# A hybrid encoder layer: attention stores begun by another engine, V laid out by pairs of heads, far results by heads, the gate from tanh

## The chip, the cores and the metric

The kernel runs on one core of one Trainium2 chip. A core has five engines with an instruction queue each, worked off in order: TensorE (PE; matmuls, its weight loads shown as PEld), VectorE (DVE), ScalarE (ACT), GpSimd (POOL) and SyncE (SP, which here only begins transfers). They wait for one another through semaphores. Sixteen DMA engines move the data; a transfer is begun by an instruction in the queue of SP, ScalarE or GpSimd. The metric is the time of one execution on the device in microseconds, lower is better.

## The reference

One layer over x (2048 positions by 1024), float32, weights and mem (256 by 1024) given:

```python
def reference(x, mem, ...):                       # one layer (DEPTH = 1)
    y = rmsnorm(h, norm_mix_g) @ w_in             # 1024 -> q 512, k 512, v 512, a 512, g 512
    q, k = partial_rotary(q), partial_rotary(k)   # 8 heads of 64
    att = dilated_sliding_attention(q, k, v)
    conv = conformer_conv(a, g, conv_w, conv_b, conv_ln_g, conv_ln_b)
    h = h + concatenate([att, conv]) @ w_out
    h = h + cross_attention(rmsnorm(h), rmsnorm(mem)) @ w_xo
    h = h + square(relu(rmsnorm(h) @ w_up)) @ w_down
    return rmsnorm(h, norm_final_g)

# dilated_sliding_attention: three patterns (128, 1), (512, 4), (2048, 16): every d-th
# position, a band of 64 to either side; outputs mixed by the softmax of their log-denominators
# conformer_conv: u = a * sigmoid(g); depthwise convolution of 31 taps + bias; layernorm; silu
```

## The kernel before, in words

Matmuls in full precision are three products of high and low halves (`mm3`, L197 to L200): a value is rounded by ScalarE to the high half, the rest is subtracted by VectorE or GpSimd. So one weight tile means a load of 512 KB, a cast on ScalarE (L189), a subtraction (L190), and 24 matmuls of 128x512 per output tile.

The order of the program is this. First mem is projected and x is normalised and transposed, all in 512-position quarters n or p. Then the input projection follows, unit by unit: `glu(c, ns)` makes channels c of the gated values (a ScalarE sigmoid of g at L508, a VectorE product with a at L511, stored to `uscr`), `lin_qk` stores q and k to scratch in DRAM, and `lin_v` writes V: for each 128 positions and each half g of the heads a tile `vst` of 4 heads x 130 numbers (64 high, two ones, 64 low) goes to the scratch `vtok`, whose rows are 8 x 130 half-precision numbers. `edges` writes zero rows ahead of it and behind it.

Then comes the *far stretch*: the attention of the first quarter, `att(0, p2_)`. There `att_far` does the distance-16 pattern for all 2048 positions, head by head, and `att_units` the two near patterns (distance 4, then distance 1) of the first quarter; heads go in pairs `pr`, `hh` is the head within a pair. One unit is: scores (PE, L855/L856 or L992), mask and row minimum (DVE, L772), Exp (ACT, L773), transposition (PE, L779), cast to a high part `ph` (ACT, L782), low part `pl` (DVE, L783), product with V (PE, L787 to L789). The units are woven as a pipeline by `att` and `weave`, with the gates of the other half of the positions (`glu(c, (2, 3))`, in `rest`) and the conv layernorm of the first quarter, whose Silu is at L266, between them. The far results (64 numbers, denominator, minimum: ROW = 66) go from `o2` to `oscr[pr][1]` once per half head, those of distance 4 from `os_` to `oscr[pr][0]` once per pair; both stores stand in ScalarE's queue (`nc.scalar`). `combine` loads both into `ld`, mixes the three patterns (mostly on GpSimd, at the end on VectorE) and transposes the result for the output projection.

After the far stretch the rest of the layer (`post(p)`: output projection, cross-attention, MLP, final norm) runs quarter by quarter, and beside it, woven in by step rates (0.95 and 0.6 a step), the near attention `att(p + 1)` and the convolution `conv(p + 1)` of the next quarter; `load_v` then loads a pattern's V tile for the next pair as soon as the old one is used up, in the far stretch all three at once after the last near unit of a pair. In the near-only quarters `turned` reorders q on GpSimd (L820).

The order on the engines is made by the framework when the program is built, from its own estimate of the times (`schedule_with_timeline_sim`); `after` and `pinned` fix parts of it: what is traced within a pinned generator is issued behind the last instruction recorded for that engine, so TensorE's order follows the order in which the generators are traced. Tiles with the same tag share buffers; a tile waits for the last reader of its buffer, a store among them. `o1` has one buffer in `aq`, and in the far stretch a second one for even pairs.

Of the kernel before, what the change touches and what calls it, by code (L numbers as in the profile page):

```python
# [10 lines left out]
F32 = mybir.dt.float32  # L11
# [10 lines left out]
P = 128  # L22
# [25 lines left out]
def hybrid_layer(ctx, tc, A, out):  # L48
# [61 lines left out]
    vtok = dr.tile([256 + S + 256, VR], F16, name="vtok")  # L110
# [3 lines left out]
    oscr = [[dr.tile([S, 2 * ROW], F32, name=f"oscr{p}_{q}") for q in (1, 2)] for p in range(4)]  # L114
# [30 lines left out]
    def setup():  # L145
# [14 lines left out]
        ACT.copy(cw.rearrange("p a b -> p (a b)"), pv[:, 64:192])  # L160
# [330 lines left out]
    def glu(c, ns, fine=False):  # L491

        sig = {}

        def unit(x, c0):
# [5 lines left out]
            for n in ns:  # L501
# [4 lines left out]
                if x == "g":  # L506
                    sig[n] = t2(f"sig{c}_{n}")
                    ACT.activation(sig[n], pt, AF.Sigmoid)  # L508
                else:
                    u = t2(f"u{c}_{n}")  # L510
                    last["dve"] = DVE.tensor_tensor(u, pt, sig[n], op=ALU.mult)  # L511
# [32 lines left out]
    def lin_v(g, ns):  # L544
# [18 lines left out]
        for t in range(4 * ns[0], 4 * ns[-1] + 4):  # L563
# [272 lines left out]
    def att_far(p2_, h, k, vt, q):  # L836
# [5 lines left out]
        def unit(rq, qh, ql):  # L842
# [40 lines left out]
    def combine(p, pr, o0):  # L883
# [63 lines left out]
    def att_units(p, far, then):  # L947
# [8 lines left out]
        def load_v(pr, pats):  # L956
            es = slice(pr * 2 * VW, (pr + 1) * 2 * VW)
            if 2 in pats and far:
                vt[2] = far.tile([P, 16, 2 * VW], F16, tag="v3", name=f"v3_{pr}")
                dma(vt[2], vtok[256:256 + S, es].rearrange("(i r) e -> i r e", r=16))  # L960
            if 0 in pats:
                vt[0] = aq.tile([P, 5, 2 * VW], F16, tag="v1", name=f"v1_{p}{pr}")
                for c in range(5):
                    t0 = 256 + 512 * p + P * c - 64
                    dma(vt[0][:, c], vtok[t0:t0 + P, es].rearrange("(i r) e -> r i e", r=16))
            if 1 in pats:
                vt[1] = aq.tile([P, 4, 2, 2 * VW], F16, tag="v2", name=f"v2_{p}{pr}")
# [467 lines left out]
```

## Time and profile before

| | |
|---|---|
| median of 3 runs | 2909.81 us (2908.92 to 2911.87) |
| the profiled execution | 2913.75 us, its span 2912.0 us |
| busy: PE, PEld | 2840.1 us (98%), 2383.9 us (82%) |
| busy: DVE, ACT, POOL | 1860.9 us (64%), 1185.7 us (41%), 456.9 us (16%) |
| DMA packets, bytes | 622,271, 433.73 MB; 553,817 of them under 2 KB, 191,269 under 512 B |
| mean granted TensorE clock | 0.990 |

The span is the time from the first to the last instruction; the execution's time holds some 2 us more. Busy time of PE is modelled from pipelined matmuls, so a busy PE is not PE at its peak. The granted clock is the share of full speed that TensorE was given. A wait is put down to what ended it last; "ACTq" and "SPq" are the instruction queues of ScalarE and SyncE where they begin a transfer.

### The profile page before, as it was taken

What the parts mean: (1) busy time and instruction counts of PE and PEld (TensorE: products, weight loads), DVE (VectorE), ACT (ScalarE), POOL (GpSimd) and SP (SyncE); (2) the same over time, 40 slices, a digit from 0 to 9 for tenths busy, and PEclk for the clock granted to TensorE, in tenths of its full rate; (3) what the DMA queues carried; (4) which work ended last, traced back from release to release, by engine and by line L of the source; (5) the groups of instructions that cost most, each with busy time, mean ns of one, the idle gap of its engine ahead of it and who ended that gap; (6) DMA issues with size and microseconds to landing.
All of it is one profiled execution on the core that took longest, in us unless ns stands there. A gap on an engine that the chain in (4) does not pass through costs nothing.

```text
span 2912.0 us, 41370 instructions
## 1 busy us (share of the span) xinstructions
PE 2840.1 (98%) x15628; PEld 2383.9 (82%) x15628; DVE 1860.9 (64%) x3311; ACT 1185.7 (41%) x2002; POOL 456.9 (16%) x502
## 2 busy tenths in 40 slices
PE   8989999989899999999999999999999999999999
PEld 7878899877688888888878888888888888888888
DVE  5636536455679886566887856589886555544445
ACT  5623211566444433433543334344333433432233
POOL 1336421121101111200021122001111200000000
PEclk9999999999899999999999999999999999999999
DMA  8979854798834544545344545534543445233332
GB/s 264 301 153 226 199 138 135 176 231 214 203 113 131 138 126 125 171 143 173 111 135 126 148 115 171 177 116 126 137 126 112 141 130 180 88 94 94 99 96 73
DMA packets 622271, 433.73 MB, mean 149 GB/s; under 512 B 191269, under 2 KB 553817, under 8 KB 622072
## 3 DMA queue, kind: packets, MB, share of 16 engines
q1 hardware_dynamic: 566904, 408.81, 50.1%
q10 hardware_dynamic: 55168, 22.29, 3.3%
q8 instruction: 123, 2.02, 0.3%
q14 instruction: 76, 0.62, 0.1%
HBM read 339.89 MB, written 91.11 MB: 148 GB/s over the span
## 4 chain that ended last, share of the span: by engine, by line
PE 82%; DVE 7%; DMA 4%; ACT 2%; issue 2%; SPq 1%; POOL 0%; ACTq 0%; POOLq 0%; DVEq 0%
PE dn L198 8%; PE dn L199 8%; PE dn L200 8%; PE up L198 7%; PE up L200 7%; PE up L199 7%; PE lin L198 3%; PE lin L199 3%; PE lin L200 3%; PE xs L198 2%; PE xs L200 2%; PE xs L199 2%; DVE cacc L215 2%; PE o L198 2%; PE o L199 2%
## 5 line engine op out<-in xcount | busy, mean ns | idle before, releaser
L199 PE MATMUL dn<-hhl,whi_d 128*128 128x512 f32 (+1 forms) x1056 | 402.9, 384 | 1.4 <-DVE hhl L1309 1.4
L198 PE MATMUL up<-mh,whi_u 128*128 128x512 f32 x1024 | 402.7, 393 | 0.8 <-DVE rl L1306 0.5
L198 PE MATMUL dn<-hhh,whi_d 128*128 128x512 f32 (+1 forms) x1056 | 401.6, 391 | 1.1 <-ACT hhh L1308 1.1
L200 PE MATMUL dn<-hhh,wlo_d 128*128 128x512 f32 (+1 forms) x1056 | 402.1, 384 | 0.0
L199 PE MATMUL up<-ml,whi_u 128*128 128x512 f32 x1024 | 399.7, 390 | 1.8 <-DVE ml L1199 1.8
L200 PE MATMUL up<-mh,wlo_u 128*128 128x512 f32 x1024 | 399.8, 391 | 0.0
L215 DVE SCALAR_TENSOR_TENSOR cacc<-cu,cw,cacc 128x512 f32<-128x512 f32 x480 | 388.8, 810 | 5.5
L189 ACT CAST whi_d<-raw_d 128x1024 fp32r<-128x1024 f32 x128 | 134.6, 1052 | 423.5 <-PE up L199 383.0
L1324 DVE TENSOR_TENSOR h<-h,dn 128x512 f32<-128x512 f32 (+1 forms) x264 | 172.3, 667 | 161.0 <-PE dn L200 159.7
L189 ACT CAST whi_u<-raw_u 128x1024 fp32r<-128x1024 f32 x128 | 134.4, 1050 | 327.6 <-PE dn L199 293.4
L1306 DVE SCALAR_TENSOR_TENSOR rl<-up,ssumx 128x512 f32<-128x512 f32 x128 | 88.0, 690 | 259.6 <-PE up L200 255.5
L198 PEld LDWEIGHTS dn<-hhh,whi_d 128*128 128x128 f32 x1056 | 197.7, 188 | 40.6 <-DVE h L1324 3.5
L200 PEld LDWEIGHTS dn<-hhh,wlo_d 128*128 128x128 f32 x1056 | 198.4, 188 | 39.3
L199 PEld LDWEIGHTS dn<-hhl,whi_d 128*128 128x128 f32 x1056 | 198.8, 188 | 37.8 <-DVE hhl L1309 2.3
L199 PEld LDWEIGHTS up<-ml,whi_u 128*128 128x128 f32 x1024 | 192.4, 188 | 41.1 <-DVE ml L1199 3.1
L200 PEld LDWEIGHTS up<-mh,wlo_u 128*128 128x128 f32 x1024 | 192.2, 188 | 40.1
L198 PEld LDWEIGHTS up<-mh,whi_u 128*128 128x128 f32 x1024 | 192.4, 188 | 39.2 <-DVE rl L1306 0.9
L773 ACT ACTIVATE sm<-sm,o 128x256 f32<-128x256 f32 (+1 forms) x384 | 160.3, 465 | 119.1 <-DVE o L772 107.4
L190 DVE TENSOR_TENSOR wlo_u<-raw_u,whi_u 128x1024 fp32r<-128x1024 f32 x128 | 162.6, 1270 | 28.7 <-ACT whi_u L189 28.4
L190 DVE TENSOR_TENSOR wlo_d<-raw_d,whi_d 128x1024 fp32r<-128x1024 f32 x128 | 160.1, 1251 | 23.7 <-ACT whi_d L189 23.5
L772 DVE CUSTOM_DVE_ANT_0 sm<-s,mask 128x256 f32<-128x256 f32 (+1 forms) x384 | 128.2, 374 | 67.3 <-PE s L992 37.5
L783 DVE TENSOR_TENSOR pl<-pt,ph 128x512 f16<-128x512 f32 x160 | 109.5, 686 | 61.6 <-ACT ph L782 60.9
(402 smaller groups left out, 6269.3 us busy)
## 6 DMA issues: line engine op xcount, KB each, us to landing
raw_u<-in_w_up_dram SPq DMA_DIRECT2D x128, 512.0 KB
raw_d<-in_w_down_dram SPq DMA_DIRECT2D x128, 512.0 KB
raw_o<-in_w_out_dram SPq DMA_DIRECT2D x32, 512.0 KB
raw_a<-ascr SPq DMA_DIRECT2D x32, 512.0 KB
raw_b<-bscr SPq DMA_DIRECT2D x32, 512.0 KB
v<-vtok SPq DMA_DIRECT2D x208, 65.0 KB
k<-kscr SPq DMA_DIRECT2D x24, 512.0 KB
k<-kscr SPq DMA_DIRECT2D x8, 1152.0 KB
```

The source lines that it names most:

```text
L189: ACT.copy(hi, raw)
L190: (lo_eng or DVE).tensor_tensor(lo, raw, f(hi), op=ALU.subtract)
L198: PE.matmul(o, lh, rh, start=first, stop=False)
L199: PE.matmul(o, lh, rl, start=False, stop=False)
L200: last["pe"] = PE.matmul(o, ll, rh, start=False, stop=end)
L215: DVE.scalar_tensor_tensor(acc, u[:, t:t + 512], cw[:, c, t:t + 1], acc, op0=ALU.mult, op1=ALU.add)
L772: last["dve"] = DVE.tensor_tensor_reduce(dst, so, mask[:, 256 * m:256 * m + nk], 1.0, 3e38, ALU.add, ALU.min, mn)
L773: last["act"] = ACT.activation(dst, dst, AF.Exp, bias=mn, scale=-1.0)
L783: DVE.tensor_tensor(pl, pt, ph, op=ALU.subtract)
L1306: last["dve"] = DVE.scalar_tensor_tensor(r, pt, 0.0, rsb, op0=ALU.max, op1=ALU.mult)
L1324: last["dve"] = DVE.tensor_tensor(hs[m][:, sl], hs[m][:, sl], pt, op=ALU.add)
```

## The change

Four things are changed. (1) In the far stretch the stores of far and distance-4 results are begun by GpSimd in place of ScalarE. (2) `vtok` is laid out as four blocks, one for each pair of heads, with rows of 2 x 130 numbers; so the distance-16 tile of a pair is loaded in one contiguous run per partition, the distance-4 tile in two transfers in place of eight (its buffer has its two middle axes swapped), the distance-1 tile as before in five; and in the far stretch each pattern's tile is loaded as soon as the old one is used up. (3) The far results get a scratch of their own, `ofar`, with a block per head; `combine` loads them with a transfer per head (three loads in place of two) and takes one step more in the later quarters. (4) The sigmoid is made from tanh: sigmoid(g) = (1 + tanh(g / 2)) / 2; the one is added in VectorE's product, the half is put into the taps of the convolution.

```diff
-    vtok = dr.tile([256 + S + 256, VR], F16, name="vtok")
+    vtok = dr.tile([H // 2, 256 + S + 256, 2 * VW], F16, name="vtok")
...
-    oscr = [[dr.tile([S, 2 * ROW], F32, name=f"oscr{p}_{q}") for q in (1, 2)] for p in range(4)]
+    oscr = [dr.tile([S, 2 * ROW], F32, name=f"oscr{p}_1") for p in range(4)]
+    ofar = [dr.tile([2, S, ROW], F32, name=f"oscr{p}_2") for p in range(4)]
...
-        ACT.copy(cw.rearrange("p a b -> p (a b)"), pv[:, 64:192])
+        ACT.activation(cw.rearrange("p a b -> p (a b)"), pv[:, 64:192], AF.Copy, scale=0.5)
...
-                    ACT.activation(sig[n], pt, AF.Sigmoid)
+                    ACT.activation(sig[n], pt, AF.Tanh, scale=0.5)
                 else:
                     u = t2(f"u{c}_{n}")
-                    last["dve"] = DVE.tensor_tensor(u, pt, sig[n], op=ALU.mult)
+                    last["dve"] = DVE.scalar_tensor_tensor(u, sig[n], 1.0, pt, op0=ALU.add, op1=ALU.mult)
...
-            s2 = st.rearrange("p h e -> p (h e)")
-            gs = slice(g * 4 * VW, (g + 1) * 4 * VW)
-            dma(vtok[256 + P * t:256 + P * (t + 1), gs], s2)
+            dma(vtok[2 * g:2 * g + 2, 256 + P * t:256 + P * (t + 1)].rearrange("r t e -> t r e"),
+                st.rearrange("p (r h) e -> p r (h e)", r=2))
...
-        zrow = wp.tile([16, 1, VR], F16, tag="raw", name="zrow", bufs=2)
+        zrow = wp.tile([64, 1, VR], F16, tag="raw", name="zrow", bufs=2)
         DVE.memset(zrow, 0.0)
-        zb = zrow.to_broadcast([16, 16, VR])
+        zb = zrow.to_broadcast([64, 4, VR])
         for t0 in (0, 256 + S):
-            dma(vtok[t0:t0 + 256].rearrange("(q x) e -> q x e", q=16), zb)
+            dma(vtok[:, t0:t0 + 256].rearrange("r (q x) e -> q r (x e)", q=64), zb)
...
-    def att_far(p2_, h, k, vt, q):
+    def att_far(p2_, h, k, vt, q, done):
...
             if rq % 2:
-                dma(oscr[pr][1].rearrange("(p r) (h e) -> p r h e", r=16, h=2)[:, 4 * rq - 4:4 * rq + 4, hh], o2,
-                    nc.scalar)
+                dma(ofar[pr][hh].rearrange("(p r) e -> p r e", r=16)[:, 4 * rq - 4:4 * rq + 4], o2, POOL)
+            if rq == 3:
+                done()
...
         ld = aq.tile([P, 2, 4, 2, ROW], F32, tag="ld", name=f"ld{p}{pr}")
-        for i in range(2):
-            dma(ld[:, i].rearrange("p j h e -> p j (h e)"),
-                oscr[pr][i][512 * p:512 * (p + 1)].rearrange("(j p) e -> p j e", p=P))
-        yield
-        yield
+        ts = slice(512 * p, 512 * (p + 1))
+        dma(ld[:, 0].rearrange("p j h e -> p j (h e)"), oscr[pr][ts].rearrange("(j p) e -> p j e", p=P))
+        for hh in range(2):
+            dma(ld[:, 1, :, hh], ofar[pr][hh, ts].rearrange("(j p) e -> p j e", p=P))
+        yield
+        yield
+        if p:
+            yield
...
         def load_v(pr, pats):
-            es = slice(pr * 2 * VW, (pr + 1) * 2 * VW)
             if 2 in pats and far:
                 vt[2] = far.tile([P, 16, 2 * VW], F16, tag="v3", name=f"v3_{pr}")
-                dma(vt[2], vtok[256:256 + S, es].rearrange("(i r) e -> i r e", r=16))
+                dma(vt[2].rearrange("i r e -> i (r e)"), vtok[pr][256:256 + S].rearrange("(i r) e -> i (r e)", r=16))
...
-                vt[1] = aq.tile([P, 4, 2, 2 * VW], F16, tag="v2", name=f"v2_{p}{pr}")
+                vt[1] = aq.tile([P, 2, 4, 2 * VW], F16, tag="v2", name=f"v2_{p}{pr}")
                 for c in range(2):
-                    src = vtok[512 * (p + c):512 * (p + c) + 512, es].rearrange("(i a b) e -> b a i e", a=4, b=4)
-                    for b in range(4):
-                        dma(vt[1][:, b, c], src[b])
+                    dma(vt[1][:, c].rearrange("p b e -> p (b e)"),
+                        vtok[pr][512 * (p + c):512 * (p + c) + 512].rearrange("(i a b) e -> a i (b e)", a=4, b=4))
...
             if g and hh and pat:
-                dma(oscr[pr][0][512 * p:512 * (p + 1)].rearrange("(p b) e -> p b e", b=4),
-                    os_.rearrange("p b h e -> p b (h e)"), nc.scalar)
+                dma(oscr[pr][512 * p:512 * (p + 1)].rearrange("(p b) e -> p b e", b=4),
+                    os_.rearrange("p b h e -> p b (h e)"), POOL if far else nc.scalar)
...
                 if pr < H // 2 - 1:
-                    if not far:
-                        load_v(pr + 1, (pat,))
-                    elif not pat:
-                        load_v(pr + 1, (2, 1, 0))
+                    load_v(pr + 1, (pat,))
...
-                    yield from att_far(far, h, k, vt, q3)
+                    yield from att_far(far, h, k, vt, q3, lambda: load_v(pr + 1, (2,)) if hh and pr < H // 2 - 1 else None)
```

More of the change, by code (lines that the diff above doesn't have):

```diff
@@ L956, in load_v @@
         def load_v(pr, pats):
-            es = slice(pr * 2 * VW, (pr + 1) * 2 * VW)
             if 2 in pats and far:
                 vt[2] = far.tile([P, 16, 2 * VW], F16, tag="v3", name=f"v3_{pr}")
-                dma(vt[2], vtok[256:256 + S, es].rearrange("(i r) e -> i r e", r=16))
+                dma(vt[2].rearrange("i r e -> i (r e)"), vtok[pr][256:256 + S].rearrange("(i r) e -> i (r e)", r=16))
             if 0 in pats:
                 vt[0] = aq.tile([P, 5, 2 * VW], F16, tag="v1", name=f"v1_{p}{pr}")
+                t0 = 256 + 512 * p - 64
                 for c in range(5):
-                    t0 = 256 + 512 * p + P * c - 64
-                    dma(vt[0][:, c], vtok[t0:t0 + P, es].rearrange("(i r) e -> r i e", r=16))
+                    dma(vt[0][:, c], vtok[pr][t0 + P * c:t0 + P * c + P].rearrange("(i r) e -> r i e", r=16))
             if 1 in pats:
-                vt[1] = aq.tile([P, 4, 2, 2 * VW], F16, tag="v2", name=f"v2_{p}{pr}")
+                vt[1] = aq.tile([P, 2, 4, 2 * VW], F16, tag="v2", name=f"v2_{p}{pr}")
                 for c in range(2):
-                    src = vtok[512 * (p + c):512 * (p + c) + 512, es].rearrange("(i a b) e -> b a i e", a=4, b=4)
-                    for b in range(4):
-                        dma(vt[1][:, b, c], src[b])
+                    dma(vt[1][:, c].rearrange("p b e -> p (b e)"),
+                        vtok[pr][512 * (p + c):512 * (p + c) + 512].rearrange("(i a b) e -> a i (b e)", a=4, b=4))
         def unit(pr, hh, pat, g, k, q_, opt, o0):
@@ L1004, in unit @@
                 for c in range(2):
-                    vv = vt[1][:, blk, c] if pat else vt[0][:, blk + c]
+                    vv = vt[1][:, c, blk] if pat else vt[0][:, blk + c]
                     att_pv(opt[0][:, blk], ph[:, 2 * z + c], pl[:, 2 * z + c], vv[:, hh * VW:(hh + 1) * VW],
```

## The prediction

> **What bounds the kernel now.** I read the page's first line, then TensorE's busy time by stages, then, inside the one stage with holes, the timeline of each engine around every hole. The row of the page and the table by stretches (columns: stretch; its length; busy us and instructions of PE, PEld, DVE, ACT, POOL; granted clock; DMA share; GB/s):
>
> ```profile
> span 2912.0 us, 41370 instructions
> 250.00:535.00 285.00, 285.00 (x1628) 251.68 (x1627) 147.05 (x209) 60.09 (x106) 91.66 (x105) 1.00 0.69 170
> 535.00:800.00 265.00, 232.26 (x1880) 197.31 (x1879) 148.99 (x569) 162.39 (x352) 44.48 (x62) 0.94 0.85 206
> 800.00:2850.00 2050.00, 2042.72 (x10462) 1688.26 (x10461) 1398.65 (x2261) 816.62 (x1276) 229.41 (x262) 1.00 0.44 130
> ```
>
> TensorE is the bound: no hole from 250 to 535, 7.3 us in the 2050 us after 800. The far stretch (the attention of the first 512 positions with the distance-16 pattern, 535 to 800) has 32.7 us of holes, and its clock of 0.94 costs about 0.06 x 265 = 16 us more. Nearly every edit acts there. Its TensorE order is written out (the sides are pinned behind the last matmul traced), so a hole closed there moves all later work forward: behind it TensorE has nothing else to wait for.
>
> **Part 1, tanh for sigmoid.** In the stretch the table loads are (groups by line; count, then busy us and mean ns), and once around a gate, ScalarE in time (start, duration):
>
> ```profile
> L773 ACT ACT_TABLE_LOAD x8 | 10.3, 1283 | 0.1
> L508 ACT ACT_TABLE_LOAD x6 | 7.7, 1283 | 0.1
> L266 ACT ACT_TABLE_LOAD x1 | 1.3, 1283 | 0.4 <-ACT o L867 0.4
> 711.54 1.28 ACT L508 ACT_TABLE_LOAD   x1
> 712.84 0.60 ACT L508 ACTIVATE sig<-lin 128x512 f32<-128x512 f32 x1
> 713.46 1.28 ACT L773 ACT_TABLE_LOAD   x1
> ```
>
> Each gate swaps Exp's table out and in: two loads, 2.57 us, in which no softmax runs. If tanh is served by Exp's table, the six gates here lose both loads, and one L773 load left from the gates before the stretch goes too: 13 x 1.283 = 16.7 us of ScalarE. The pair at Silu (L266 and its way back) stays. What TensorE lost around the six gates:
>
> ```profile
> 543.00:547.00 4.00, 3.11 (x30) 2.58 (x30) 2.00 (x10) 3.96 (x6) 0.00 (x0) 1.00 0.72 182
> 562.00:567.00 5.00, 3.15 (x29) 2.49 (x28) 4.04 (x13) 4.96 (x10) 0.96 (x1) 1.00 1.09 292
> 622.00:626.00 4.00, 3.48 (x31) 2.64 (x30) 1.84 (x10) 3.02 (x9) 0.00 (x0) 1.00 1.19 249
> 638.00:647.00 9.00, 6.08 (x38) 5.00 (x37) 3.03 (x11) 6.33 (x12) 2.11 (x1) 0.81 0.50 116
> 691.00:701.00 10.00, 8.02 (x65) 6.41 (x64) 3.38 (x13) 7.22 (x12) 0.00 (x0) 0.83 0.54 145
> 711.00:721.00 10.00, 8.60 (x58) 6.80 (x57) 5.28 (x25) 7.69 (x16) 0.00 (x0) 0.83 0.64 148
> ```
>
> Length less PE busy, summed: 42.00 - 32.44 = 9.6 us of holes. The clock falls behind the longer ones: (1 - clock) x length is 1.7 us in each of the last three, 5.1 us. Together 14.7. What comes late next is VectorE's low part of the probabilities behind ScalarE's cast, which I take at half a microsecond a place: 14.7 - 6 x 0.5 = **11.7 us gained** (bounds 0, if the order only shifts, and 14.7). The Trainium skill, ScalarE: Activation LUTs, section "Table sets", lists tanh among the companions of exp, so that one load would serve both; no tanh is in this trace.
>
> The arithmetic itself costs nothing new:
>
> ```profile
> L511 DVE TENSOR_TENSOR u<-lin,sig x16: 616/692/693, 155.0 to 744.9; 128x512 f32<-128x512 f32 x16
> L1306 DVE SCALAR_TENSOR_TENSOR rl<-up,ssumx 128x512 f32<-128x512 f32 x128 | 88.0, 690 | 259.6 <-PE up L200 255.5
> ```
>
> The product becomes a scalar_tensor_tensor of the same shape from PSUM, 692 against 690 ns; the halving of the taps rides in a copy that is there already (L160), once. If VectorE's cover went, 16 x some ns would be under 1 us.
>
> **Part 2, the far stretch's stores from GpSimd.** ScalarE at one store, and the chain of waits for the same place:
>
> ```profile
> 612.93 0.37 ACT L867 COPY o<-opt 128x260 f32<-128x260 f32 x1
> 617.13 0.37 ACTq L57 DMA_DIRECT2D oscr<-o  x1
> 617.54 0.59 ACT L782 CAST ph<-pt 128x512 f16<-128x512 f32 x1 [4.23 <-DMA ql<-qfar]
> ...
> 610.36 6.70 DMA ql<-qfar
> ```
>
> The store takes 0.37 us to issue, but is held for 4 us until a load that it shares no data with has landed, and the probabilities' casts queue behind it on ScalarE. Three such holds reach TensorE:
>
> ```profile
> 615.00:622.00 7.00, 4.88 (x30) 3.90 (x29) 1.80 (x6) 4.41 (x6) 5.48 (x6) 0.76 1.03 251
> 671.00:676.00 5.00, 3.52 (x30) 2.54 (x29) 2.20 (x7) 3.34 (x7) 4.06 (x4) 1.00 1.06 229
> 746.00:756.00 10.00, 6.35 (x30) 4.70 (x30) 3.45 (x8) 3.98 (x8) 0.00 (x0) 0.66 1.18 207
> ```
>
> Holes 2.1 + 1.5 + 3.6 = 7.2 us; clock 0.24 x 7 = 1.7 and 0.34 x 10 = 3.4, of which about 1 us fell into holes: 4.1. Together 11.3, less 0.5 in three places: 9.8. On GpSimd a held store blocks combine's products, the low weight halves of the gates (L190) and `turned` (L820); GpSimd is busy 44 of 265 us, so short holds cost nothing, and if that cover went a gate's matmuls would wait for `wlo`. No row shows a GpSimd store. I take three quarters, **7.3 us gained** (bounds: 0, the hold only moves, and 11.3).
>
> The Trainium skill, DMA: Bandwidth & Descriptors, section "Issuing engines are not separate DMA queues", says that choosing another engine saves only the issue time, usually small. Here that would be 20 x 0.37 = 7.4 us of ScalarE, spread in pieces too short to open a hole, so nearly nothing on TensorE; the 4.23 us hold is time in ScalarE's queue that this rule does not count. It is the first rival below.
>
> **Part 3, what the transfers carry.** In 535 to 800 (queue: packets, MB, share of 16 engines; issues):
>
> ```profile
> q1 hardware_dynamic: 59700, 48.84, 74.4%
> q10 hardware_dynamic: 17216, 5.41, 10.2%
> oscr<-o ACTq DMA_DIRECT2D x20, 264.0 KB
> v<-vtok SPq DMA_DIRECT2D x52, 65.0 KB
> v<-vtok SPq DMA_DIRECT2D x3, 1040.0 KB
> ```
>
> q10 carries ScalarE's stores. A far store is 128 x 8 pieces of 264 bytes; by heads the 8 rows of a partition lie together, 128 pieces of 2112 bytes. The distance-16 load goes from 2048 pieces of 520 bytes to 128 of 8320; the eight distance-4 loads of a pair become two, in pieces of 2080 bytes. The four near stores' 4 x 512 pieces stay, so 10.2% of the DMA engines falls to perhaps 3 (by packets, (2048 + 2048) / 17,216 of it, and a little for the longer pieces), and v's 52 x 128 + 3 x 2048 = 12,800 packets of q1's 59,700 to about a third. SP issues 14 - 8 = 6 v loads fewer a pair and one `ld` load more. I add no gain for this: with DMA share 0.85, one hole in the stretch waits for a v load (next part). The earlier v3 load (after the last far product rather than behind the near ones) acts on the same wait. After 800 TensorE has 7.3 us of holes in all, so 7 v loads a pair instead of 13 change nothing there; nor do `combine`'s extra step and the third `ld`, unless `cath` came late for the next block's output matmuls. The V store goes from 1040- to 520-byte pieces in a stretch without a hole (250 to 535, six buffers); without those, ScalarE's V cast would wait. The zero rows keep 2080-byte pieces. The 64-row memset has the same columns. All nothing.
>
> **Part 4, the junction.** The last pair's near store is on the path: the next block's first softmax takes the same buffer.
>
> ```profile
> 742.51 6.42 DMA qh<-qscr
> ...
> 768.46 4.92 DMA oscr<-o
> ...
> 774.95 7.24 DMA raw_o<-in_w_out_dram
> ...
> 774.98 0.20 PE L789 MATMUL opt<-v,pl 128*128 128x65 f16 x1 [3.65 <-DVE pl L783]
> 770.00:780.00 10.00, 6.35 (x32) 4.72 (x31) 5.76 (x21) 1.61 (x5) 0.00 (x0) 0.83 0.67 179
> 777.99 3.13 SPq L57 DMA_DIRECT2D v<-vtok  x5
> 783.12 0.19 PE L787 MATMUL opt<-v,ph 128*128 128x65 f16 x1 [1.45 <-DMA v<-vtok]
> 784.54 1.20 POOL L820 CAST qt<-qh 128x512 fp32r<-128x512 f32 x1 [21.18 <-DMA qh<-qscr]
> 785.69 1.09 POOL L820 CAST ql<-ql 64x512 fp32r<-64x512 f32 x1
> ```
>
> The store lands 4.92 us after its issue, and each later microsecond is one of TensorE. From GpSimd: at best equal, at worst as long again (+5); I take +1.5, near the low end, as bytes and pieces are the same. Five v loads take SP 3.13 us here; with six of thirteen gone, the 1.45 us hole at 783 mostly closes: -0.5 to -1.5, I take -0.5. Net **+1.0**. The Trainium skill, DMA: Bandwidth & Descriptors, "Specifications", gives a first byte after about 1 us from GpSimd and 0.6 from SP or ScalarE: by that the store would be 0.4 us later; no run here shows it.
>
> Silu's hole stays:
>
> ```profile
> 583.00:599.00 16.00, 12.74 (x98) 10.05 (x97) 8.41 (x33) 13.00 (x24) 2.60 (x2) 0.89 1.03 279
> ```
>
> **Sum.** -11.7 - 7.3 + 1.0 = -18.0 us. The profiled execution took 2913.75 us (span 2912.0 and 1.75 around it), 3.9 above the median of 2909.81; so 2895.8 beside it, **2891.8 beside the median**, taken as 2892.
>
> **The rivals.**
> - *The holds only move* (the Trainium skill's rule above). For: a hold waits for another transfer, and GpSimd's queue may be held likewise, with the landing late. Against: the load it waited for was SP's, and the casts are no longer behind it. Then -11.7 + 1.0: 2899. Chance 0.16.
> - *Tanh needs a load of its own*, so the loads stay: -7.3 + 1.0: 2903.5. Nothing in the trace speaks for or against. 0.06.
> - *The junction takes it back*: in the chain from 742 to 782 the landings of 6.42, 4.92 and 7.24 us are the longest pieces beside the wait for GpSimd, and if these come no earlier, the far stretch ends sooner and waits longer there. Against: those loads wait for buffers that the far stretch frees, so they move with it. A quarter remains, -4.5: 2905. 0.10.
> - *Slower: the last near store stands behind `turned` in GpSimd's queue.* GpSimd works in order; the second `turned` sat 21.18 us waiting for its load and ended at 786.8. A store behind it would begin there instead of at 768.46: 18.3 us late, with the `ld` load, combine and the first output matmuls that need its result after it. With the full gain that is 2910, no change; with the first rival's gain -10.7 + 18.3: 2917. It decides from a delay of 18 + 6 = 24 us with the full gain. For: the queue's order is the planner's. Against: the store is ready 16 us before that load. 0.13, other bad orders of GpSimd's queue included.
>
> **How the numbers follow.** My forecast 0.55. A difference under 0.2% (5.8 us) can't be told from none. Faster: 0.55 + 0.16 + 0.06 = 0.77; same 0.10; slower 0.13. The likeliest case alone spans 2882 (14.7 + 11.3 + 1.5 = 27.5 gained) to 2899. The range leaves out the slower case and a twentieth below, where smoother transfers also close the small holes: 2880 to 2910.
>
> **What would show it.** Right: no table load at L508, and one at L773 in the stretch, behind Silu; holes of 535 to 800 down from 32.7 to 18 to 22 us, clock 0.96 or more; no DMA issue on ScalarE there and no 4 us idle before its casts; q10 near nothing; DMA share under 0.8. Wrong: loads at L508, GpSimd stores that take several us, a longer landing at the junction's store, or new holes in 535 to 800 whose releaser is GpSimd.

## The result, and the profile after

The changed kernel takes 2904.64 us in the median of 18 runs (2899.87 to 2909.61), the kernel before, on the same chip, 2909.1: a ratio of 0.9983, 95% interval 0.9976 to 0.9991. That is 4.5 us gained (by the interval 2.6 to 7.0) where 18 were forecast. Line numbers of the changed kernel stand one above those of before (L773 is the old L772); `combine`'s first operation, `csm`, is L903 before and L908 after.

Stages of the changed kernel (columns as in the prediction: busy us and instructions of PE, PEld, DVE, ACT, POOL; clock; DMA share; GB/s), and the row of the kernel before that the prediction did not show:

```profile
150.00:250.00 100.00, 95.63 (x439) 78.91 (x438) 43.03 (x55) 37.06 (x58) 53.64 (x42) 0.98 0.80 189
250.00:535.00 285.00, 283.03 (x1618) 249.93 (x1617) 142.22 (x205) 57.80 (x102) 89.61 (x102) 1.00 0.67 168
535.00:800.00 265.00, 233.18 (x1928) 203.31 (x1927) 158.70 (x580) 151.21 (x346) 53.37 (x81) 0.94 0.81 215
800.00:2850.00 2050.00, 2039.00 (x10446) 1684.08 (x10446) 1385.14 (x2253) 810.91 (x1269) 231.98 (x262) 1.00 0.43 129
```
```profile
150.00:250.00 100.00, 90.80 (x407) 74.40 (x406) 38.85 (x51) 33.30 (x54) 49.50 (x38) 0.93 0.80 178
```

The far stretch has as many holes as before (31.8 us in 265; 32.7 before), the stage from 150 to 250 has 4.8 us fewer, the one from 250 to 535, which had none, has 2.0, the long stage behind has 3.7 more. How much time each part took is read better from two events: the first far score and the first output matmul behind the junction. Before (span 2912.0), then after (span 2901.6), from the timeline of TensorE:

```profile
538.61 0.28 PE L855 MATMUL s<-k,qh 128*128 128x256 f32 x1
...
787.63 0.80 PE L198 MATMUL o<-cath,whi_o 128*128 128x512 f32 x1 [0.78 <-ACT cath L941]
```
```profile
535.38 0.28 PE L856 MATMUL s<-k,qh 128*128 128x256 f32 x1
...
773.37 0.80 PE L199 MATMUL o<-cath,whi_o 128*128 128x512 f32 x1 [0.78 <-ACT cath L946]
```

So the start of the far stretch comes 3.2 us earlier, the far stretch takes 238.0 us in place of 249.0, and the rest 2128.2 in place of 2124.4. (Of the 10.4 us between these two spans a part is that the profiled execution of before stood 3.9 us over the median; a second profile of the changed kernel, e13 below, in an execution 8 us over its median, has 242.7 and 2130.8.)

Between the two events the same 1818 matmuls keep TensorE busy for 216.3 us before and 206.2 after, with holes of 32.7 and 31.8 us. So by the profile the far stretch is shorter because its matmuls take less time, not because holes closed. The granted clock does not account for it (0.94 before, 0.95 after; 0.92 in e13, whose matmuls there take 209.0 us), and the runs don't show what does.

What TensorE waited for from 535 to 800 (columns: us, times, longest), before and after:

```profile
PE opt L789 <- DVE pl L783: 11.9, 16, 3.6
PE pt L779 <- ACT sm L773: 11.2, 9, 2.4
PE opt L787 <- ACT ph L782: 4.7, 6, 1.9
PE opt L787 <- DMA v<-vtok: 1.5, 1, 1.5
```
```profile
PE opt L790 <- DVE pl L784: 16.4, 14, 5.4
PE opt L788 <- DMA v<-vtok: 6.2, 1, 6.2
PE catT L944 <- DVE cat L936: 4.4, 1, 4.4
PE opt L788 <- ACT ph L783: 2.1, 2, 1.2
PE pt L780 <- ACT sm L774: 0.8, 1, 0.8
```

The holes that ScalarE ended went as forecast, from 15.9 to 2.9 us (11.2 + 4.7, then 2.1 + 0.8). In their place come VectorE's low part and, at the junction, a V load and `combine`. VectorE was late because it works in order and stood in front of `csm` until `combine`'s loads had landed (groups by line, 535 to 800; the last column is the idle time before), before and after:

```profile
L903 DVE TENSOR_TENSOR csm<-ld 128x8 f32<-128x8 f32 x4 | 0.7, 172 | 1.2 <-DMA ld<-oscr 1.2
```
```profile
L908 DVE TENSOR_TENSOR csm<-ld 128x8 f32<-128x8 f32 x4 | 0.7, 173 | 17.7 <-DMA qh<-qfar 9.3 <-DMA v<-vtok 8.4
```

The chain of waits to the longest of these holes, after:

```profile
633.68 8.85 DMA oscr<-o
642.53 0.01 issue
642.55 7.39 SPq L57
...
651.07 6.95 DMA qh<-qfar
658.02 0.04 issue
658.06 0.18 DVE csm L908
...
659.47 0.61 DVE pl L784
660.08 0.05 issue
660.13 0.23 PE opt L790
```

A store begun by GpSimd lands 8.85 us after its issue; SP, which has waited for it, is then held 7.39 us at the `ld` load, right behind the far keys' load of 1.1 MB; the loads issued there land 7 us later (the profile puts the wait down to one of them, `qh`; `csm` itself reads `ld`), and `csm`, a softmax and `pl` follow one another.

Two things the prediction had called nothing stand in the other stages: the shorter hole at 206, and three new holes of 2.4 us, one at the turn of each two later quarters.

### The profile page after: what moved, and what is told of

It reads as the page before. It is cut to its first block, busy times and chain, and to the rows that moved or that the text cites. A ratio compares the mean times of both kernels' runs of the same rounds, so it can differ in the third digit from the quotient of the medians.

```text
span 2901.6 us, 41366 instructions
## 1 busy us (share of the span) xinstructions
PE 2829.1 (97%) x15628; PEld 2379.8 (82%) x15628; DVE 1850.8 (64%) x3311; ACT 1166.3 (40%) x1988; POOL 470.3 (16%) x522
## 3 DMA queue, kind: packets, MB, share of 16 engines
q0 software_dynamic: 1600, 5.41, 0.5%
## 4 chain that ended last, share of the span: by engine, by line
PE 86%; DMA 5%; DVE 5%; issue 2%; ACT 1%; SPq 1%; POOL 0%; POOLq 0%; DVEq 0%; ACTq 0%
PE up L199 8%; PE up L200 8%; PE up L201 8%; PE dn L199 8%; PE dn L200 8%; PE dn L201 8%; PE lin L199 3%; PE lin L201 3%; PE lin L200 3%; PE o L199 2%; PE o L201 2%; PE o L200 2%; PE xs L199 2%; PE xs L201 2%; PE xs L200 2%; PE pt L780 2%
## 5 line engine op out<-in xcount | busy, mean ns | idle before, releaser
L1306 DVE SCALAR_TENSOR_TENSOR rl<-up,ssumx 128x512 f32<-128x512 f32 x128 | 88.1, 690 | 251.3 <-PE up L201 247.1
L199 PEld LDWEIGHTS dn<-hhh,whi_d 128*128 128x128 f32 x1056 | 197.7, 188 | 47.6 <-DVE h L1324 11.9
L773 DVE CUSTOM_DVE_ANT_0 sm<-s,mask 128x256 f32<-128x256 f32 (+1 forms) x384 | 128.4, 374 | 72.4 <-PE s L995 29.3
L177 POOL TENSOR_TENSOR nr<-st_v,mhalf 128x4 f32<-128x4 f32 (+1 forms) x13 | 13.0, 996 | 906.5 <-DVE st_v L173 906.5
```

The source lines that it names most:

```text
L177: POOL.tensor_tensor(dst, v, mhalf.to_broadcast([P, v.shape[1]]), op=ALU.pow)
L199: PE.matmul(o, lh, rh, start=first, stop=False)
L773: last["dve"] = DVE.tensor_tensor_reduce(dst, so, mask[:, 256 * m:256 * m + nk], 1.0, 3e38, ALU.add, ALU.min, mn)
L1306: last["dve"] = DVE.scalar_tensor_tensor(r, pt, 0.0, rsb, op0=ALU.max, op1=ALU.mult)
```

## The experiments

The theory at the start: the parts on ScalarE gain what was forecast, and `combine`'s late loads on VectorE (L) or the new order of the V loads (V) take it back. All results, each ratio against runs of the kernel before on the same chip, with the three times taken from the same two TensorE rows and the span of each profile; the intervals make a difference of two ratios uncertain by some 0.0017, 5 us. The three times are of one execution each: the two profiles of the changed kernel (changed, e13) differ in them by 6.2, 4.7 and 2.6 us, so a smaller difference between two rows says nothing. "Fixes" are the later `combine` and the short V loads of the text below.

| kernel | ratio to before | first far score | far stretch | rest |
|---|---|---|---|---|
| before | 1 | 538.6 | 249.0 | 2124.4 |
| changed | 0.9983 (0.9976-0.9991) | 535.4 | 238.0 | 2128.2 |
| e1 before + tanh | 0.9969 (0.9957-0.9980) | 537.0 | 242.8 | 2122.6 |
| e2 before + GpSimd stores | 0.9999 (0.9990-1.0008) | 537.2 | 245.1 | 2123.2 |
| e3 before + both | 0.9965 (0.9953-0.9978) | 537.4 | 239.0 | 2125.1 |
| e4 changed, ScalarE stores | 1.0027 (1.0016-1.0039) | 537.0 | 248.8 | 2130.2 |
| e5 changed, later combine | 0.9955 (0.9942-0.9969) | 539.0 | 225.8 | 2132.3 |
| e6 changed, old V order | 1.0006 (0.9997-1.0014) | 540.1 | 245.9 | 2132.3 |
| e7 changed, far results by pairs, no step | 1.0034 (1.0024-1.0045) | 539.5 | 246.6 | 2131.1 |
| e8 changed, no extra step | 0.9995 (0.9984-1.0006) | 538.0 | 237.4 | 2134.2 |
| e9 before + zero rows | 0.9981 (0.9972-0.9990) | 534.2 | 251.3 | 2123.6 |
| e10 e3 + zero rows + later combine | 0.9953 (0.9940-0.9965) | 531.2 | 243.9 | 2124.7 |
| e11 changed, short V loads | 0.9928 (0.9915-0.9940) | 538.8 | 235.1 | 2120.1 |
| e12 changed, both fixes | 0.9890 (0.9875-0.9905) | 535.9 | 221.8 | 2120.4 |
| e13 changed, again | 0.9988 (0.9979-0.9997) | 541.6 | 242.7 | 2130.8 |
| e14 e12, ScalarE stores | 0.9944 (0.9932-0.9956) | 538.4 | 239.2 | 2120.0 |
| e15 e12, short loads in quarter 1 too | 0.9882 (0.9869-0.9896) | 535.9 | 225.8 | 2120.1 |
| e16 e12, far results by pairs | 0.9937 (0.9923-0.9950) | 542.2 | 233.6 | 2120.7 |
| e17 e15, V as before | 0.9888 (0.9873-0.9903) | 533.8 | 223.8 | 2122.6 |
| e18 e15, old V order | 0.9870 (0.9852-0.9888) | 532.3 | 222.7 | 2119.1 |

**Tanh alone (e1).**

```diff
-                    ACT.activation(sig[n], pt, AF.Sigmoid)
+                    ACT.activation(sig[n], pt, AF.Tanh, scale=0.5)
-                    last["dve"] = DVE.tensor_tensor(u, pt, sig[n], op=ALU.mult)
+                    last["dve"] = DVE.scalar_tensor_tensor(u, sig[n], 1.0, pt, op0=ALU.add, op1=ALU.mult)
```


> The kernel before with the gate from tanh alone. Theory A (the tables were worth what I predicted, and something else of the change takes it back): the loads at L508 and L773 go, 11.7 us gained, 0.9960 of the kernel before. Theory B (the order only shifts: the softmax behind the gate waits for VectorE's work instead): 5 us or less, 0.9983 or more. Theory C (tanh needs a table of its own): 1.000, and 13 loads in the far stretch stay. The trace of the whole change speaks against C.

0.0031 x 2914 us = 9.0 us gained (5.8 to 12.5): theory A. The same 1631 matmuls, from the first far score to just ahead of the held store at 748 (740 in e1), before and in e1 (columns as in the stages):

```profile
538.61:748.00 209.39, 186.90 (x1631) 161.29 (x1629) 118.22 (x494) 137.52 (x307) 37.65 (x57) 0.96 0.86 210
```
```profile
537.02:738.00 200.98, 181.68 (x1631) 157.83 (x1629) 117.95 (x494) 121.24 (x295) 37.62 (x57) 0.98 0.89 218
```

This part is 8.4 us shorter: 3.2 of it are holes (22.5 to 19.3), 5.2 shorter matmuls. At that held store TensorE's wait for Exp grew from 2.34 to 4.61 us. In the changed kernel the stretch from 535 to 800 has two table loads left, those around Silu:

```profile
L267 ACT ACT_TABLE_LOAD x1 | 1.3, 1283 | 0.0
L774 ACT ACT_TABLE_LOAD x1 | 1.3, 1283 | 0.0
```

**GpSimd stores alone (e2), and both (e3).**

```diff
-                dma(oscr[pr][1]...[:, 4 * rq - 4:4 * rq + 4, hh], o2, nc.scalar)
+                dma(oscr[pr][1]...[:, 4 * rq - 4:4 * rq + 4, hh], o2, POOL)
...
-                    os_.rearrange("p b h e -> p b (h e)"), nc.scalar)
+                    os_.rearrange("p b h e -> p b (h e)"), POOL if far else nc.scalar)
```


> The kernel before with the 20 stores of the far stretch begun by GpSimd, nothing else. Theory A: the three holes behind a held ScalarE store go, 7.3 us gained, 0.9975. Theory B (the holds only move, since the landing from GpSimd of 4 to 9 us makes combine's load late): 0.999 to 1.002, with VectorE standing before the first operation of combine (csm) for some 3 us a pair.

> Tanh and the GpSimd stores on the kernel before; V's scratch, its loads and the far results stay as they were. Theory A: 18 us gained, 0.994, so that the new layout and its load order cost some 13 us of the whole change's 4.5. Theory B: these two parts already give only what the whole change gives, 4 to 6 us, 0.998, and the layout is worth nothing either way.

Nothing alone (0.9999): theory B of e2. With tanh the two give 10.2 us, 1.2 beyond tanh alone; that lies between the two theories of e3 (18 us, and 4 to 6), and the rest of the change takes back some 5 us on balance. TensorE's waits of e2 from 535 to 800, and VectorE's in front of `csm`:

```profile
PE opt L789 <- DVE pl L783: 11.1, 17, 1.4
PE pt L779 <- ACT sm L773: 8.6, 6, 2.4
PE opt L787 <- DMA v<-vtok: 5.8, 1, 5.8
PE opt L787 <- ACT ph L782: 3.7, 5, 1.2
```
```profile
L903 DVE TENSOR_TENSOR csm<-ld 128x8 f32<-128x8 f32 x4 | 0.7, 172 | 5.9 <-DMA ld<-oscr 5.9
```

ScalarE's holes fell by 3.6 us (15.9 to 12.3). The holes behind VectorE outside the junction rose from 8.3 (11.9 less the 3.65 at 775) to 11.1, and the junction kept its 6 us under another name (a V load for 3.65 + 1.45 + 1.08). The hold has moved from ScalarE to VectorE.

**The changed kernel with its stores back on ScalarE (e4).**

> The changed kernel with its 20 stores of the far stretch back on ScalarE. Theory A (the stores on GpSimd are worth 7.3 us): 7 us slower than the changed kernel, 1.0008 of the kernel before. Theory B (GpSimd's late landings hold up combine's loads, and so cost what they save): same as the changed kernel, 0.998, or up to 5 us faster, 0.9965; then the holds in front of combine on VectorE are shorter than the changed kernel's 3.7, 6.3 and 3.0 us.

12.8 us slower than the changed kernel (11.4 by e13): theory A by its sign, and more than it asked. So the same stores are worth nothing in the kernel before and a lot in the changed one; which of the other edits makes the difference this run does not show.

**Later combine (e5).**

```diff
-            for _ in range(2 if pr < 3 else 1):
+            for _ in range(4 if pr < 3 else 1):
```


> The changed kernel with combine's first operation two steps later for the first three pairs of the first quarter (4 steps in place of 2), so that its loads have about 10 us more. Theory L (VectorE's 17.7 us in front of csm take back the gain): that wait falls below 6 us, the holes at 607, 660 and 711 (9 us together) mostly close, 6 us faster than the changed kernel, 0.996 of the kernel before. Theory V (the lost time is the load queue's, and only changes its place): holes of the same size for another load, 0.998.

8 us faster than the changed kernel: theory L. VectorE's wait in front of `csm` falls from 17.7 to 5.8 us, the far stretch from 238.0 to 225.8.

**Old place of the V loads (e6), far results by pairs (e7), no extra step (e8).**

```diff
 # e6
-                    load_v(pr + 1, (pat,))
+                    if not far:
+                        load_v(pr + 1, (pat,))
+                    elif not pat:
+                        load_v(pr + 1, (2, 1, 0))
 # e7: oscr[pr][1] and two ld loads as in the kernel before; e8:
-        if p:
-            yield
```


> The changed kernel with the next pair's V loads of the first quarter back at their old place (all three behind the last near product), layout and sizes as in the change. Theory V (the early distance-16 and distance-4 loads push the far keys, and with them combine's loads, back): the hold behind the far keys falls from 7 to 9 us to 4, 5 us faster than the changed kernel, 0.9965 of before. Theory L (combine's loads are late in any order once the stores come from GpSimd): same as the changed kernel, 0.998.

> The changed kernel with the far results back by pairs of heads (two loads in combine, 264-byte pieces in the far stores) and without combine's extra step in the later quarters; V's layout and loads as in the change. Theory F (the third load and the step cost): the three holes of 2.4 us at the turns of the quarters go and the junction loses one load, 6 us faster than the changed kernel, 0.996. Rival (only the step matters): 4 us at most, and the same as the kernel without the step. Theory V: same as the changed kernel, 0.998.

> The changed kernel without combine's extra step in the later quarters, nothing else. If the step moves the turns of the quarters so that a softmax stands 5.4 us in front of the last near store's landing: the holes of 2.4 us at 1101, 1647 and 2193 go, 4 us faster than the changed kernel (0.997 of before). If the third load is what moves them: same as the changed kernel, and the holes stay.

Theory V falls: with the old place it is 5 to 7 us slower, which theory L did not say either. F falls too, and so do its two rivals: by pairs it is some 11 us slower than e8, which lacks the step as well. The step itself is worth nothing that can be told (0.9995 against 0.9983 and 0.9988), and the holes at the turns stay without it (7.4 us in e8). The third load does not make them either: e7 has only two, and 6.4 us there. All three have long rests (2131 to 2134 us), as has every kernel with the long distance-4 loads.

**Zero rows (e9).**

```diff
-        zrow = wp.tile([16, 1, VR], F16, tag="raw", name="zrow", bufs=2)
+        zrow = wp.tile([64, 1, VR], F16, tag="raw", name="zrow", bufs=2)
...
-            dma(vtok[t0:t0 + 256].rearrange("(q x) e -> q x e", q=16), zb)
+            dma(vtok[t0:t0 + 256].rearrange("(q x) e -> q x e", q=64), zb)
```


> The kernel before with only the zero rows around V written from 64 partitions (4 rows each) instead of 16 (16 rows each); same bytes, same 2080-byte pieces, no other part of the change. Theory Z (the zero rows are what the x tiles' stores queue behind, and cost TensorE 8 us at 206): the two holes there fall from 9.2 to about 4.5 us, 4 to 5 us gained, 0.9984. My prediction's own term: nothing, 1.000, and the shorter hole in the changed kernel comes from V's stores or from chance.

5.5 us gained (2.9 to 8.2): theory Z. The list of four changes does not name this edit, though the diff has it. TensorE's wait for the x tiles from 150 to 250 (us, times, longest), before and in e9:

```profile
PE xt L332 <- DVE xv L337: 9.2, 2, 8.0
```
```profile
PE xt L332 <- DVE xv L337: 4.9, 2, 2.6
```

The chain of waits from the second write of zero rows on (start, duration), before and in e9:

```profile
180.97 12.44 DMA vtok<-zrow
...
193.48 0.39 SPq L57
```
```profile
182.27 7.07 DMA vtok<-zrow
...
189.42 0.39 SPq L57
```

The zero rows stand in a buffer that the next weight load takes (both have the tag `raw`, with two buffers), so SP begins nothing more until they have landed. From 16 partitions the second half megabyte lands after 12.44 us, from 64 after 7.07: 5.4 us, the whole gain. Everything in SP's queue moves forward by that much, the stores of the x tiles among it, and TensorE waits less for the buffers that they free.

**Parts added up on the old layout (e10).**

> On the kernel before: tanh, the GpSimd stores, the zero rows from 64 partitions, and combine's first operation two steps later in the first quarter; V's scratch, its loads and the far results as before. If the parts add up (10 for tanh and stores, 4.5 for the zero rows, 5 to 8 for the later steps): 19 to 22 us gained, 0.993. If the new layout was needed for combine's loads to be in time: 0.9955, as the changed kernel with the later steps.

Only 0.9953: the parts do not add up. It is the time of the other theory but not its reason: VectorE's wait in front of `csm` is 5.5 us, as short as in e5. TensorE waits 13.1 us for V loads from 535 to 800 (1.5 before); between 600 and 680, where the DMA engines are full (share 1.02), it waits 4.9 us for them and 3.6 for the far queries.

**Short V loads in the later quarters (e11), and both fixes (e12).**

```diff
-                    dma(vt[1][:, c].rearrange("p b e -> p (b e)"), ...)      # 260 KB, twice
+                    for b in range(4):
+                        dma(vt[1][:, c, b], src[b])                            # 65 KB, eight times; not if far
```


> The changed kernel with the distance-4 V load of the later quarters in eight transfers of 65 KB again instead of two of 260 KB. Theory Q (at the turn of two quarters the two long loads go ahead of the last near store, which then lands 7.2 us after its issue instead of 4.3, and a softmax, with TensorE behind it, waits for that): the holes of 2.4 us at 1101, 1647 and 2193 close, 5 us faster than the changed kernel, 0.9965 of before. Rival (the turn's order itself is what changed): same as the changed kernel, 0.998, and the holes stay.

> The changed kernel with both: combine two steps later in the first quarter, and the eight shorter V loads in the later quarters. If both theories hold they add, 8 + 5 = 13 us below the changed kernel, 0.9938 of before. If the turn's holes are not the loads': as the later steps alone, 0.9955.

Theory Q, three times as large as put: 16 us (17.5 by e13). The turn of two quarters, the changed kernel and then e11:

```profile
1088.29 1.14 SPq L57 DMA_DIRECT2D v<-vtok  x2
1089.10 0.33 ACTq L57 DMA_DIRECT2D oscr<-o  x1
...
1096.37 0.42 DVE L773 CUSTOM_DVE_ANT_0 sm<-s,mask 128x256 f32<-128x256 f32 x1 [5.38 <-DMA oscr<-o]
...
1100.74 0.50 PE L199 MATMUL dn<-hhh,whi_d 128*128 128x512 f32 x1 [2.44 <-DVE h L1324]
```
```profile
1087.69 5.41 SPq L57 DMA_DIRECT2D v<-vtok  x8
1088.51 0.33 ACTq L57 DMA_DIRECT2D oscr<-o  x1
...
1092.47 0.42 DVE L773 CUSTOM_DVE_ANT_0 sm<-s,mask 128x256 f32<-128x256 f32 x1 [2.08 <-PE s L1000]
```

The store's buffer `o1` is the next softmax's. With two long loads, 520 KB are queued ahead of the store, and VectorE gets past its wait 7.3 us after the store's issue; with eight, SP takes 5.41 us to issue them, the store goes in between, and the softmax starts 4.0 us after the store's issue, released by its scores. The rest falls from 2128.2 to 2120.1 us; it is 2128 to 2134 in all seven kernels that have the long loads there and 2119 to 2125 in the other thirteen. At the junction, where the second quarter's first V tile is loaded, the wait for `combine` goes too, in e11 from 535 to 800:

```profile
PE opt L788 <- DMA v<-vtok: 4.6, 1, 4.6
PE catT L944 <- DVE cat L936: 0.2, 1, 0.2
```

The changed kernel had 6.2 and 4.4 there; the seven kernels with the long loads have 3.9 to 4.5 us in the second row, none of the others has more than 0.2. Together with the later `combine` it is 0.9890, 27 us faster than the changed kernel.

**The changed kernel again (e13), and parts taken away from e12 (e14 to e16).** The edits of e14 and e16 are those of e4 and e7 (the step stays); e15 drops the exception for `far` in e11's edit.

> The changed kernel itself, on the same chip and beside the same runs of before as the next three. If the eight shorter loads and the later steps are worth what the runs before say, it stays at 0.998 (0.997 to 0.999) and the sum of its parts closes: tanh 9, zero rows 5.5 gained, the rest of it 10 lost. If the chips differ, it comes out near 0.995, and the two fixes are worth less.

> The kernel with both fixes (combine two steps later in the first quarter, eight short V loads in the later quarters), with the 20 stores back on ScalarE. Theory A (GpSimd's stores are worth the holds of ScalarE as soon as combine no longer waits): 7 to 12 us slower than with both fixes, 0.992. Theory B (the holds only move): same as with both fixes, 0.989.

> The kernel with both fixes, and the distance-4 V loads in eight pieces in the first quarter too. If the two long loads are what helps the far stretch (fewer issues on SP ahead of the keys): 3 to 6 us slower, 0.9905. If long loads are bad there too (they go ahead of what is waited for): 3 us faster, 0.988.

> The kernel with both fixes, with the far results back by pairs of heads (264-byte pieces in the far stores, two loads in combine; the extra step stays). If the far results by heads are worth something by themselves (the stores land in 5.8 us in place of 7.2): 3 to 10 us slower, 0.991. If they only made combine's loads less late: same as with both fixes, 0.989.

The changed kernel keeps its ratio (0.9988). The GpSimd stores are worth 15.7 us in e12: theory A. Back on ScalarE, TensorE waits for Exp again, here e14 from 535 to 800:

```profile
PE pt L780 <- ACT sm L774: 10.4, 5, 6.5
```

The far results by heads are worth 13.7 us. Long loads in the first quarter gain nothing (0.9882 without, 0.9890 with), and every kernel that has them has a hole of 2 to 4 us at about 510, where TensorE waits for the low half of V (`vst`) on VectorE; none that lacks them has it. From 250 to 535 TensorE is busy 283.12 of 285 us in e12 and all 285.00 in e15.

**V's layout and the place of its loads (e17, e18).** e17 is e15 with V's scratch, its loads and their place as in the kernel before; e18 is e15 with e6's edit.

> The kernel with combine two steps later and all distance-4 loads in eight pieces (0.9882), but V's scratch by tokens and the V loads at their old place, as in the kernel before; tanh, GpSimd stores, far results by heads and the zero rows from 64 partitions stay. If the V layout with its long distance-16 load and its earlier place is worth the step from 0.9953 (tanh, stores, zero rows, later combine) to 0.9882: 0.994 to 0.995. If the far results by heads are worth that step: 0.988 to 0.989.

> The kernel with combine two steps later and all distance-4 loads in eight pieces (0.9882), V's layout as changed, but all V loads of the first quarter at their old place behind the last near product. If the earlier place is worth something by itself: 3 to 8 us slower, 0.990 or more. If only the layout counts: 0.988.

With V wholly as before it is 0.9888, with the new layout and the old place 0.9870, with the new place 0.9882: by the intervals neither the V scratch nor the earlier place is worth anything that can be told. But e17 and e18 ran side by side, and all four times of e18 (2874.70 to 2878.11 us) lie below all four of e17 (2879.95 to 2882.41): there the new layout, with its loads at the old place, is worth some 6 us. The step from e10 to e17, the far results by heads and `combine`'s step, is worth 19 us. The stretch from 600 to 680, e10 and e17:

```profile
600.00:680.00 80.00, 67.97 (x595) 58.93 (x594) 40.67 (x175) 42.19 (x104) 24.29 (x40) 0.91 1.02 227
```
```profile
600.00:680.00 80.00, 76.97 (x732) 68.86 (x731) 50.27 (x210) 51.74 (x128) 24.32 (x43) 1.00 1.03 262
```

The queue of GpSimd's stores in the same 80 us (packets, MB, share of 16 engines), e10 and e17:

```profile
q0 software_dynamic: 558, 1.88, 9.6%
```
```profile
q0 software_dynamic: 683, 2.34, 8.3%
```

Both fill the DMA engines; with pieces of 2112 bytes in place of 264 (by the kernels' layouts; the packets that the profile counts for this queue hold some 3.4 KB in both) the stores take 3.5% a megabyte in place of 5.1, all queues together move 262 GB/s in place of 227, and TensorE does 732 matmuls in place of 595. The Trainium skill, DMA: Bandwidth & Descriptors, section "Specifications", names 512 bytes as the least transfer for full rate; these rows agree with it in direction, but no run here tries a size near 512.

The fastest kernel is e18: tanh, GpSimd stores, far results by heads with `combine`'s extra step, V by pairs of heads with its loads at the old place, zero rows from 64 partitions, `combine` two steps later in the first quarter, eight short distance-4 loads. It takes 2875.58 us where before took 2915.44, a ratio of 0.987 (0.9852 to 0.9888); by the ratio 38 us.

## Why the prediction failed

The ladder, each step in us of 2914: tanh -9.0; the GpSimd stores -1.2 (e3); zero rows and later `combine` -3.5 (e10); far results by heads -18.9 (e17); V by pairs and its earlier loads -1.7 (e15); long distance-4 loads: in the first quarter +2.3 (e12), in the later ones +18.9 (e5); `combine` early again +8 to +10 (the changed kernel). It ends at -3.5 to -5.0, the measured time. The steps depend on their order: what relieves one engine shows only when the next is not late.

- **Part 1 was right in its time**, a little too large: -11.7 forecast, -9.0 measured, within its bounds. The loads went, and the product of 128x512 stayed at 0.69 us or less. By the rule of the Trainium skill, ScalarE: Activation LUTs, "Table sets", tanh needs no load of its own; the trace agrees: 15 table loads from 535 to 800 before, 2 after, both around Silu. The second rival falls with it. Ahead of the junction its split came out otherwise: 6.6 us of holes were put (9.6 less 3.0) and 3.2 came, 5.1 us of clock were put and the matmuls took 5.2 less; 2.3 were lost again at the next held store (e1).
- **Part 2 is one step that failed**: it took three quarters of three holes, "7.3 us gained", as if the stores' worth were fixed. On the kernel before they gave 0.3 us alone and 1.2 beyond tanh: the first rival, in its pure form. The lower bound, 0, said that the hold might only move, but not where to. The place was VectorE, which in the order of before stood only 1.2 us at `csm`. It is not a rule, though: taken out of the changed kernel the same stores are worth 11 to 13 us (e4), out of e12 15.7, twice the term. The Trainium skill, DMA: Bandwidth & Descriptors, section "Issuing engines are not separate DMA queues" (only the issue is saved) fits e2 and not e4 and e14; the hold on ScalarE is real, but its worth depends on who waits next.
- **Part 3 is the other, and the larger**: "I add no gain for this", "so 7 v loads a pair instead of 13 change nothing there", "All nothing". Four terms were hidden there: long loads in the later quarters +16 to +19, `combine` in front of late loads +8 to +11, zero rows -5.5, far results by heads -11 to -19. The first two together cost 27 us (e12 against the changed kernel), where 13.5 were missing. Two arguments were at fault. That "one hole in the stretch waits for a v load" looked at who waits for that load, not at what queues behind it; and a mean DMA share of 0.85 hid stretches that were full (the prediction's own rows show 1.03 to 1.19 in six places), where a store's efficiency moves every other load. From 7.3 us of holes after 800 it followed that little could be gained there, but a loss was possible, and was not bounded. The stores' share was also read too far from their packets: 10.2% was to fall "to perhaps 3"; in 2,880 packets in place of 17,216 it was 6.0% (e4).
- **Part 4** had +1.0 for the junction; the changed kernel lost 4.5 there (6.24 for a V load and 4.42 for `combine`, against 3.65 + 1.45 + 1.08). The near store was later by about what was put: the softmax behind it began 6.9 us after its issue (748.46 to 755.37) in place of 4.92. What was wrong is the sign for the V loads: with six of thirteen gone the hole did not close but grew, and the wait for `combine` goes with the long loads (e11).
- **The third rival** named the measured time, 2905, by luck: the junction gave back 4.5 of the 13.5 us that are missing, VectorE and the turns the most. **The slower rival** did not come: `turned` ended at 746.2 and the last near store was issued at 748.46, behind its own result.
- **What was to show it**: table loads, ScalarE's queue and `q10` came as put (the stores are in `q0` now, with 6.0%). Holes of 18 to 22 us, a clock of 0.96 and a DMA share under 0.8 did not (31.8, 0.94, 0.81). New holes were looked for behind GpSimd; they came behind VectorE and a V load. In e12 the clock is 0.96 and the holes are 17.

Open is the size of the interactions: the intervals leave each step uncertain by some 5 us, and why the old V place costs 5 to 7 us in the changed kernel and nothing in e15 was not settled beyond the longer wait at `csm` in e6 (26.7 us). Open is also whether the GpSimd stores and the far results by heads need each other: each is worth 11 us and more where the other is present, and no run has the changed kernel without both. And what makes the matmuls of the far stretch shorter is not shown.

## What to carry to other kernels

When a wait is taken from one engine, find the next instruction that waits for the same data on another engine, and ask whether everything queued behind it can spare the time; moving that waiting instruction two steps later cost one line here and gave 8 to 11 us. Fewer and longer transfers are not better by themselves: a long load that nobody needs yet goes ahead of a short store that somebody does. Where the DMA engines are full, the layout of a store can count for every transfer beside it (e17 against e10), and a mean share over a stage hides that. A load that takes the buffer of a store waits for the store to land, and so does everything behind it in its queue (the zero rows).

## What the runs showed of the hardware

- A store of 264 KB begun by GpSimd took it 0.57 us in the mean in the changed kernel (20 in 11.3 us, 16 of them in pieces of 2112 bytes) and 0.85 in e10 (20 in 17.0 us, those 16 in pieces of 264). It landed 2.4 to 8.8 us after its issue (median 5.9) in the one and 4.9 to 9.9 (median 7.1) in the other.
- The same 5.41 MB of stores begun by ScalarE took 10.2% of the DMA engines from 535 to 800 in 17,216 packets (before) and 6.0% in 2,880 (e4): a sixth of the packets, three fifths of the time.
- Two loads of 260 KB delayed the landing of a store issued behind them by about 3 us against eight loads of 65 KB (7.3 against 4.0 to 4.3). The Trainium skill, DMA: Bandwidth & Descriptors, section "Rules for kernel authors", advises to coalesce many small transfers into a large one; measured in a whole kernel, eight of 65 KB were 16 to 19 us faster than two of 260.
- The second of two writes of 520 KB of zeros landed 12.44 us after its issue from 16 partitions (before) and 7.07 from 64 (e9); why 16 are slower the runs don't show.
- The granted clock was 1.00 between 600 and 680 in e17, where TensorE had 3.0 us of holes, and 0.91 in e10, where it had 12.0, at the same DMA share (1.03 and 1.02).
